# Two wide output projections: from three column pieces of 384, 384 and 256 to two of 512

## The chip, the cores and the metric

The kernel runs on one core of a Trainium2 chip. The metric is the device time of one execution in microseconds (us). Besides the timed runs there is one execution taken by the hardware profiler; its rows are what every argument here goes by.

Engines are named as the profile names them: PE is the matrix engine (TensorE) and PEld its weight loads, ACT is ScalarE, DVE is VectorE, POOL is GpSimd, SP is the engine whose queue issues nearly all transfers.

## The reference, cut to what matters

One step of an encoder layer for 1024 prompt tokens and 64 sample tokens, width 1024, all in float32:

```
h   = rms_norm(x, n_pre)
aq, af, ai, ag, bq, bk, bv, bg, cu, cg = split(h @ w_in)
a_out = rms_norm(hgrn2_scan(aq, af, ai)) * silu(ag)        # width 512
b_out = stick_breaking_attention(bq, bk, bv) * silu(bg)    # width 256
c_out = pool_mix(cu) * silu(cg)                            # width 256
mix = concat(a_out, b_out, c_out) @ w_out                  # 1024 x 1024
x   = x + rms_norm(mix, n_post)
q   = rms_norm(x, nx_pre) @ w_xq                           # 4 heads of 256
p   = softmax(q k_mem / 16) per head, over 256 memory rows
x   = x + rms_norm(concat(p v_mem) @ w_xo, nx_post)        # 1024 x 1024
```

The two "wide" products of the title are `mix @ w_out` and the last one with `w_xo`. Each maps 1088 token rows of width 1024 to 1024 columns.

## The kernel before, in words

**Precision.** A float32 product is made of three matmuls. Every operand is kept as a high part `hi` (rounded by ACT to the type float32r) and a low part `lo` (DVE subtracts `hi` from the original); the product is hi*hi + hi*lo + lo*hi, accumulated in PSUM. `mm3` issues these three for each of the 8 blocks of 128 along the inner dimension (`k`).

**Token tiles and chunks.** There are nine token tiles: eight of 128 prompt rows, and tile 8 with the 64 sample rows. In projections with the tokens as the streamed operand they go in three chunks of 384, 384 and 320 tokens (`CHUNKS`). The normalised, transposed input lies in six token buffers, a pair `hhi0..2`, `hlo0..2` of the shape 128 x 8 x n for n = 384, 384, 320. Two sets of them exist in the course of the program: one for `h`, later one for the second norm's output.

**Wide projections.** Here the tokens are the stationary operand: `side(i)` splits tile i of the mixed heads `C` into `whi`, `wlo`, and asks for the residual rows to be loaded into `C`. `wide(i)` streams the weights against them, one PSUM bank per piece of columns. The weights live in the six token buffers once the last projection of a chunk has read them: the piece of the columns 0:384 in pair 0, 384:768 in pair 1, 768:1024 in pair 2. `load_wide` fills one pair: for each block of 128 columns one transfer of 512 KB into a staging buffer `wraw` (the pool has two, shared with the norms), one ACT copy (hi), one DVE subtraction (lo). A tile needs 8 x 3 = 24 matmuls per piece, 72 in all. For tile 8 `whi` and `wlo` stand side by side in the 128 stationary columns, so it takes two matmuls per `k`, 48 in all. `wide_norm` then reads each piece from PSUM: an ACT square with a sum per row, a DVE multiplication by the gain; POOL adds the pieces' sums and makes the reciprocal root; DVE adds the result to the residual in `C`.

**Where this stands.** `w_out` is loaded during the last keys/values block of the stick-breaking attention (`keys_values`, j = 1), chunk by chunk; its tiles run partly between the attention's last units (task "sb", names `sm`, `wT`, `vb`) and mostly after them. `w_xo` is loaded during the last head (h = 3) of the cross attention, again chunk by chunk; its tiles are the end of the program, in the order 0 to 5, 8, 6, 7.

**What sets the order.** The program is one generator (`main`) and side tasks spawned from it. A planner (`Sched`) with a cost in us for every instruction runs the first task in its list whose inputs are ready when PE gets there; a wide projection gives way to other tasks after each six matmuls. The tile framework then places the instructions on each engine; blocks under `urgent()` have higher priority. Each engine runs its own list strictly in that order. The helper lines that carry nearly everything are `mm` (L171 before), `act` (L183), `tt` (L187), `stt` (L191) and `wload` (L286).

Of the kernel before, what the change touches and what calls it, by code (L numbers as in the profile page):

```python
# [8 lines left out]
F32 = mybir.dt.float32  # L9
# [6 lines left out]
P = 128  # L16
# [7 lines left out]
EPS = 1e-6  # L24
QSCALE = 128 ** -0.5
NEG = -1e30
PIECES = ((0, 3), (3, 6), (6, 8))
CHUNKS = ((0, 384), (384, 384), (768, 320))
URGENT = 1500
TABLE = {AF.Exp: 0, AF.Sigmoid: 2, AF.Ln: 5, AF.Silu: 18}  # L30
# [74 lines left out]
def hybrid_step(  # L105
# [627 lines left out]
    def main():  # L733
# [208 lines left out]
            yield from pooled(1, us[1])  # L942

        st, sbops = {}, {}
        wo, wdeps = [], []

        def keys_values(bi, j, wbs, q):


            kh = pool([P, KEYS], F32R, "kh", 2)  # L950
            kl = pool([P, KEYS], F32R, "kl", 2)
            ck = pool([P, P], F32, "ck", 1)
            SP.dma_start(ck, cache_sb_k[j * P:(j + 1) * P, :])
            split(ck, kh[:, SEQ:SEQ + P], kl[:, SEQ:SEQ + P])
            vb = pool([P, NT, P], F32, "vb", 2)
            cv = pool([P, P], F32, "cv", 2)
            SP.dma_start(cv, cache_sb_v[0, 0, :, 2 * j:2 * j + 2, :])
            sbops[j] = (q, (kh, kl), vb, cv)
            rows, cs = slice(j * P, (j + 1) * P), slice(j * P, (j + 1) * P)
            for c, (t0, n) in enumerate(CHUNKS):  # L960
                n1 = min(n, SEQ - t0)
                sch.fresh(**wbs[0][2])
                yield None
                yield from proj(wbs[0], c, hT)
                o = cur["o"]
                kr = pool([P, 384], F32, "kr", 3)
                with urgent():
                    split(o[:, :n1], kh[:, t0:t0 + n1], kl[:, t0:t0 + n1])
                    if n1 < n:
                        split(o[:, n1:n], kh[:, SEQ + P:], kl[:, SEQ + P:])  # L970
                    act(kr[:, :n], o[:, :n], AF.Copy)
                SP.dma_start(p_sb_k[rows, t0:t0 + n1], kr[:, :n1])
                if n1 < n:
                    SP.dma_start(s_sb_k[rows, :], kr[:, n1:n])
                sch.fresh(**wbs[1][2])
                yield None
                yield from proj(wbs[1], c, hT)
                o = cur["o"]
                vr = pool([P, 384], F32, "kr", 3)
                with urgent():  # L980
                    act(vr[:, :n], o[:, :n], AF.Copy)

                def values_tm(vr, c, t0, n, n1):
                    yield None
                    if c:
                        yield f"bv{j}{c - 1}"
                    pt = ps_tp().rearrange("p (c t) -> p c t", t=P)
                    i0, full = t0 // P, n1 // P
                    for i in range(full):
                        tr(pt[:, i, :], vr[:, i * P:(i + 1) * P], P)  # L990
                    if n1 < n:
                        tr(pt[:SMP, full, :], vr[:, n1:n], P)
                    act(vb[:, i0:i0 + full, :], pt[:, :full, :], AF.Copy)
                    SP.dma_start(p_sb_v[0, 0].rearrange("(i p) h d -> p i (h d)", p=P)[:, i0:i0 + full, cs],
                                 vb[:, i0:i0 + full, :])
                    if n1 < n:
                        act(vb[:SMP, 8, :], pt[:SMP, full, :], AF.Copy)
                        SP.dma_start(s_sb_v[0, 0].rearrange("p h d -> p (h d)")[:, cs], vb[0:SMP, 8, :])
                sch.spawn(values_tm(vr, c, t0, n, n1), f"bv{j}{c}")
                if (j, c) == (0, 0):  # L1000
                    sch.spawn(sb_all(sbops, pool), "sb")
                if j == 1:
                    b0, b1 = PIECES[c]
                    pair = [big([P, KT, n], F32R, f"{x}{c}") for x in ("hhi", "hlo")]
                    wdeps.append(load_wide(w_out, pair, range(b0, b1)))
                    wo.append((slice(b0 * P, b1 * P), *pair))
                elif c == 1:
                    prefetch(bi + 2)
                    prefetch(bi + 3)

        def load_wide(src, tiles, blocks):
            save, sch.cur = sch.cur, Sched.Task(None, "w")
            hi, lo = tiles
            for i, cb in enumerate(blocks):
                with urgent():
                    raw = wload(src[cb])
                    cs = slice(i * P, (i + 1) * P)
                    act(hi[:, :, cs], raw, AF.Copy)
                    sub(lo[:, :, cs], raw, hi[:, :, cs].bitcast(F32))
            dep, sch.cur = dict(sch.cur.dep), save  # L1020
            return dep
        for bi, (kind, j) in enumerate(names):
            if (kind, j) == ("cu", 0):
                wbs = [wq.pop(bi), wq.pop(bi + 1)]
# [175 lines left out]
                SP.dma_start(C[:n, i].rearrange("p k t -> p (k t)"), res)  # L1200
            return ahi, alo, dict(sch.cur.dep)

        def wide(i, sd, w, wdeps, bank):

            ahi, alo, dep = sd
            pp = []
            for (cs, whi, wlo), wd in zip(w, wdeps):
                sch.fresh(**dep)
                sch.cur.dep.update(wd)
                yield None  # L1210
                p = bank()
                wn = cs.stop - cs.start
                if i < 8:
                    yield from mm3(p[:, :wn], [(ahi[:, k], alo[:, k], whi[:, k, :wn], wlo[:, k, :wn])
                                               for k in range(KT)], 6)
                else:
                    for k in range(KT):
                        mm(p[:, :wn], ahi[:, k], whi[:, k, :wn], k == 0, False)
                        mm(p[:, :wn], ahi[:, k], wlo[:, k, :wn], False, k == KT - 1)
                        if k % 3 == 2:  # L1220
                            yield None
                pp.append((cs, p[:, :wn]))
            cur["pp"] = pp

        def wide_norm(i, pp, gain):
# [22 lines left out]
        for i in range(NT):  # L1248
            sch.fresh()
            yield ("sb", 0, i)  # L1250
            yield ("sb", 1, i)
            sd = side(i, xrows(i))
            if i == NT - 1:
                xw[0] = wblock(w_xq[0])
            yield from wide(i, sd, wo, wdeps, ps_mm if i < 8 else ps_hg)
            if i == NT - 1:
                xw[1] = wblock(w_xq[1])
            with urgent():
                x = wide_norm(i, cur["pp"], g2)
            SP.dma_start(x1d[i * P:i * P + _rows(i), :], x)  # L1260
            sch.done[("x1", i)] = max(sch.cur.dep.values())
            if not h2 and "sb" in sch.done:
                open_h2()
# [62 lines left out]
            sch.done[("cross", h, c)] = max(sch.cur.dep.values())  # L1326

        prev = None
        wx, wdeps = [], []
        for h in range(4):  # L1330
            def load_kv(h):
                kr = xq([P, 2, NMEM], F32, "kraw", 1)
# [16 lines left out]
            for c, (t0, n) in enumerate(CHUNKS):  # L1349
                n1 = min(n, SEQ - t0)  # L1350
                qhi = xq([P, 2, 384], F32R, "qhi", 2)
                qlo = xq([P, 2, 384], F32R, "qlo", 2)
                qs = xq([P, 2, SMP], F32, "qs", 2) if n1 < n else None
                deps = {}
                for dt in range(2):
                    sch.fresh(**wbs[dt][2])
                    yield ("h2", c)
                    yield from proj(wbs[dt], c, hT)
                    o = cur["o"]
                    with urgent():  # L1360
                        act(qhi[:, dt, :n1], o[:, :n1], AF.Copy, scale=0.0625)
                        stt(qlo[:, dt, :n1], o[:, :n1], 0.0625, qhi[:, dt, :n1].bitcast(F32), ALU.mult, ALU.subtract)
                        if n1 < n:
                            tsc(qs[:, dt, :], o[:, n1:n], 0.0625, ALU.mult)
                    if c == 2 and h < 3:
                        xw[2 * h + 2 + dt] = wblock(w_xq[2 * h + 2 + dt])
                if h == 3:
                    b0, b1 = PIECES[c]
                    pair = [h2p([P, KT, n], F32R, f"{x}{c}") for x in ("hhi", "hlo")]
                    wdeps.append(load_wide(w_xo, pair, range(b0, b1)))  # L1370
                    wx.append((slice(b0 * P, b1 * P), *pair))
                if prev is not None:
                    save = dict(sch.cur.dep)
                    yield prev
                    sch.fresh(**save)
                sch.spawn(cross(h, c, qhi, qlo, qs, kv), f"cross{h}{c}")
                prev = f"cross{h}{c}"
# [3 lines left out]
        for i in (0, 1, 2, 3, 4, 5, 8, 6, 7):  # L1381
            sch.fresh()
            yield ("cross", 3, i // 3)
            sd = side(i, x1d[i * P:i * P + _rows(i), :])
            yield from wide(i, sd, wx, wdeps, ps_mm)
            x = wide_norm(i, cur["pp"], g4)
            for cs, _ in cur["pp"]:
                SP.dma_start(yrows(i)[:, cs], x[:, cs])
# [71 lines left out]
```

## Time and profile before

| | us |
|---|---|
| three timed runs | 934.79, 938.41, 1758.64; median 938.41 |
| the profiled execution, its own time | 935.02 |
| its span, first to last instruction | 933.3 |
| outside the span | 1.7 |
| granted TensorE clock, mean | 0.996 |

One of the three runs is far off the other two; the profiled execution stands beside the lower of those two. In the rows below a time is counted in us from the span's start. Matmuls are pipelined and their ends are modelled, so the duration in a matmul's row is longer than what one costs in a stream: that is read from the starts of successive matmuls. A row of the timeline gives the start, the duration (all in us), the engine, the line, what it writes and reads, and in square brackets the idle time of the engine ahead of it with what ended it.

### The profile page before, as it was taken

To read this page: it belongs to the slowest core of one execution; us is meant where nothing else is said; L and a number is where in the kernel's file an instruction comes from. 1 tells how busy PE (TensorE), PEld (TensorE's weight loads), DVE (VectorE), ACT (ScalarE), POOL (GpSimd) and SP (SyncE) were. 2 spreads that over 40 slices of the span, in tenths; PEclk is the share of its full clock that TensorE was granted. 3 is DMA by queue.
4 is the path that set the end of the run, shared out by engine and by line. 5 is a ranking of instruction groups with operands and counts; after the bars stand their busy time and mean duration, and the time that the engine had idled before them with its cause. 6 is when DMAs were issued, how large, how long until landed. Compare 5 with 4: busy or idle time off the path is not lost.

```text
span 933.3 us, 18372 instructions
## 1 busy us (share of the span) xinstructions
PE 914.2 (98%) x7504; PEld 853.6 (91%) x7504; DVE 556.6 (60%) x1125; ACT 479.5 (51%) x1005; POOL 107.2 (11%) x194
## 2 busy tenths in 40 slices
PE   8899999999999999999999999999999999999997
PEld 7899999999998999989779788999999999999997
DVE  6849483674678574552684777565564545563343
ACT  7623384658767774963673765433452333342231
POOL 5502430010010010000000000211200000001110
PEclk9999999999999999999999999999999999999999
DMA  8815511011100111012111411222433111232231
GB/s 306 259 38 181 142 46 47 25 49 29 47 27 31 47 33 46 25 47 79 47 31 36 157 61 69 90 68 80 164 119 92 30 39 46 76 106 91 91 101 58
DMA packets 33126, 73.60 MB, mean 79 GB/s; under 512 B 5601, under 2 KB 18065, under 8 KB 33042
## 3 DMA queue, kind: packets, MB, share of 16 engines
q1 hardware_dynamic: 30112, 68.07, 22.7%
q0 software_dynamic: 1888, 4.35, 1.3%
q8 instruction: 59, 0.97, 0.4%
q14 instruction: 25, 0.20, 0.1%
q10 hardware_dynamic: 1042, 0.01, 0.1%
HBM read 56.45 MB, written 15.89 MB: 78 GB/s over the span
## 4 chain that ended last, share of the span: by engine, by line
PE 82%; DVE 6%; ACT 4%; DMA 4%; issue 2%; POOL 1%; DVEq 0%; POOLq 0%; ACTq 0%
PE mm L171 64%; PE hg L171 14%; PE tp L175 5%; DVE sm L650 3%; DVE sm L187 1%; DVE wlo L187 1%; ACT L183 1%; ACT whi L183 1%; DMA xt<-in_x_prompt_dram 1%; DVE hlo L187 1%; DMA wraw<-in_w_xk_dram 1%; DMA mkd<-mraw 1%; DMA wraw<-in_w_xo_dram 1%; DMA gT<-in_norm_mem_dram 1%; DMA mvd<-mtm 1%
## 5 line engine op out<-in xcount | busy, mean ns | idle before, releaser
L171 PE MATMUL mm<-hhi,whi 128*128 128x384 f32 (+2 forms) x1272 | 425.1, 334 | 0.0
L171 PE MATMUL mm<-hlo,whi 128*128 128x384 f32 (+2 forms) x1272 | 412.5, 325 | 0.0
L171 PE MATMUL mm<-hhi,wlo 128*128 128x384 f32 (+2 forms) x1248 | 405.3, 325 | 0.0
L171 PEld LDWEIGHTS mm<-hhi,whi 128*128 128x128 f32 x1272 | 239.2, 188 | 6.3 <-issue 1.3
L171 PEld LDWEIGHTS mm<-hlo,whi 128*128 128x128 f32 x1272 | 239.5, 188 | 1.2 <-issue 0.9
L171 PEld LDWEIGHTS mm<-hhi,wlo 128*128 128x128 f32 x1248 | 234.6, 188 | 0.4 <-issue 0.3
L187 DVE TENSOR_TENSOR wlo<-wraw,whi 128x1024 fp32r<-128x1024 f32 (+1 forms) x53 | 63.5, 1200 | 56.6 <-ACT whi L183 56.3
L183 ACT ACT_TABLE_LOAD x66 | 84.7, 1283 | 19.0 <-DVE E L187 12.0
L183 ACT ACTIVATE whi<-wraw 128x1024 fp32r<-128x1024 f32 (+1 forms) x53 | 55.3, 1043 | 71.5 <-PE mm L171 54.7
L183 ACT ACTIVATE wraw<-mm 128x384 f32<-128x384 f32 (+3 forms) x51 | 22.9, 449 | 72.8 <-PE mm L171 62.9
L650 DVE TENSOR_TENSOR_SCAN sm<-sm 128x384 f32<-128x384 f32 (+4 forms) x52 | 48.3, 938 | 14.0 <-ACT sm L183 14.0
L183 ACT ACTIVATE sm<-hg 128x384 f32<-128x384 f32 (+4 forms) x104 | 42.2, 485 | 15.7 <-PE hg L171 8.7
L187 DVE TENSOR_TENSOR wraw<-mm,gain 128x384 f32<-128x384 f32 (+1 forms) x48 | 24.4, 510 | 41.6 <-ACT wraw L183 41.3
L1241 POOL TENSOR_TENSOR small<-small 128x1 f32<-128x1 f32 (+1 forms) x18 | 4.2, 234 | 375.3 <-ACT wraw L183 375.3
L183 ACT ACTIVATE E<-E 128x512 f32<-128x512 f32 (+1 forms) x68 | 32.8, 515 | 10.5 <-DVE E L187 9.9
L171 PE MATMUL mm<-mhi,wlo 128*128 128x256 f32 x128 | 35.8, 289 | 1.8 <-DVE wlo L187 1.8
L321 POOL TENSOR_TENSOR small<-small,mhalf 128x1 f32<-128x1 f32 (+2 forms) x50 | 36.0, 719 | 4.2
L171 PE MATMUL mm<-mhi,whi 128*128 128x256 f32 x128 | 36.2, 293 | 0.1
L171 PE MATMUL mm<-mlo,whi 128*128 128x256 f32 x128 | 35.1, 283 | 0.0
L443 POOL COPY qf<-q 128x512 f32<-128x512 f32 (+1 forms) x12 | 14.6, 1218 | 177.6 <-PE hg L171 140.7
L187 DVE TENSOR_TENSOR wlo<-C,whi 128x1024 fp32r<-128x1024 f32 x16 | 19.6, 1225 | 24.9 <-ACT whi L183 23.4
L191 DVE SCALAR_TENSOR_TENSOR C<-wraw,small,C 128x384 f32<-128x384 f32 (+3 forms) x54 | 27.8, 569 | 10.2 <-POOL small L321 10.2
(209 smaller groups left out, 1409.1 us busy)
## 6 DMA issues: line engine op xcount, KB each, us to landing
wraw<-in_w_in_dram SPq DMA_DIRECT2D x28, 512.0 KB, 3.6
xt<-in_x_prompt_dram SPq DMA_DIRECT2D x8, 512.0 KB, 6.5
wraw<-in_w_xv_dram SPq DMA_DIRECT2D x8, 512.0 KB, 3.9
wraw<-in_w_out_dram SPq DMA_DIRECT2D x8, 512.0 KB, 3.6
C<-in_x_prompt_dram SPq DMA_DIRECT2D x8, 512.0 KB, 3.5
x1d<-C SPq DMA_DIRECT2D x8, 512.0 KB, 2.8
wraw<-in_w_xq_dram SPq DMA_DIRECT2D x8, 512.0 KB, 3.6
wraw<-in_w_xo_dram SPq DMA_DIRECT2D x8, 512.0 KB, 3.6
```

The lines of the kernel that those rows point to most:

```text
L171: cur['PE'] = PE.matmul(out, lhsT=lhsT, rhs=rhs, start=start, stop=stop, skip_group_check=True)
L175: PE.transpose(out, in_, ident[:n, :n])
L183: cur['ACT'] = ACT.activation(out, in_, func, **kw)
L187: cur['DVE'] = DVE.tensor_tensor(out=out, in0=a, in1=b, op=op)
L191: DVE.scalar_tensor_tensor(out=out, in0=a, scalar=s, in1=b, op0=op0, op1=op1)
L321: POOL.tensor_tensor(out=r[:n, :w], in0=r[:n, :w], in1=mhalf[:n, :w], op=ALU.pow)
L443: POOL.tensor_copy(qf[:, 1, :], qq)
L650: DVE.tensor_tensor_scan(m[:nq, :n][:, ::-1], m[:nq, :n][:, ::-1], m[:nq, :n][:, ::-1], 1.0 if p is None else p[:nq, 0:1], ALU.mult, ALU.min)
L1241: POOL.tensor_tensor(out=ms[:n, 0:1], in0=ms[:n, 0:1], in1=ms[:n, pi:pi + 1], op=ALU.add)
```

## The change

Both wide projections take two pieces of 512 columns ("halves") in place of three. A half needs 8 rows (k = 0..7) of 512 weights for the hi part and as many for the lo part; the 16 rows of the two halves are laid one behind the other into the same six token buffers. Pair 0 (8 x 384 = 6 x 512) takes the rows k = 0..5 of half 0; pair 1 the rows 6, 7 of half 0 and 0..3 of half 1; pair 2 the rows 4..7 of half 1. `ROWS` says so, as (half, k from, k to, first row in the buffer). Each entry of `ROWS` is loaded with four transfers, one per block of 128 columns, which carry only the rows of that entry: 384 KB each for pair 0, 128 KB and then 256 KB for pair 1, 256 KB for pair 2. That is 16 transfers, 16 ACT copies and 16 DVE subtractions per weight matrix where there were 8 of each, on the same number of elements. A half of tile 0 cannot end before every row of that half is there: half 0 reads pairs 0 and 1, half 1 reads pairs 1 and 2.

A tile takes 2 x 24 = 48 matmuls of 512 columns, tile 8 takes 32. `wide_norm` is unchanged but now gets two pieces: two squares, two multiplications, two residual additions, and no separate addition of sums on POOL (L1241). The results leave in two transfers per tile, not three.

```
-PIECES = ((0, 3), (3, 6), (6, 8))
+ROWS = (((0, 0, 6, 0),), ((0, 6, 8, 0), (1, 0, 4, 2)), ((1, 4, 8, 0),))
...
-        def load_wide(src, tiles, blocks):
+        def load_wide(src, w, tiles, c):
             save, sch.cur = sch.cur, Sched.Task(None, "w")
-            hi, lo = tiles
-            for i, cb in enumerate(blocks):
-                with urgent():
-                    raw = wload(src[cb])
-                    cs = slice(i * P, (i + 1) * P)
-                    act(hi[:, :, cs], raw, AF.Copy)
-                    sub(lo[:, :, cs], raw, hi[:, :, cs].bitcast(F32))
+            for half, k0, k1, r0 in ROWS[c]:
+                rows = [t.rearrange("p k n -> p (k n)")[:, r0 * 512:(r0 + k1 - k0) * 512].rearrange(
+                    "p (k n) -> p k n", n=512) for t in tiles]
+                hi, lo = rows
+                for i in range(4):
+                    with urgent():
+                        raw = wpool([P, KT, P], F32, "wraw", 2)[:, :k1 - k0]
+                        SP.dma_start(raw, src[4 * half + i][:, k0:k1])
+                        cs = slice(i * P, (i + 1) * P)
+                        act(hi[:, :, cs], raw, AF.Copy)
+                        sub(lo[:, :, cs], raw, hi[:, :, cs].bitcast(F32))
+                for k in range(k0, k1):
+                    w[half][k] = (hi[:, k - k0], lo[:, k - k0], dict(sch.cur.dep))
...
-        def wide(i, sd, w, wdeps, bank):
+        def wide(i, sd, w, bank):
             ahi, alo, dep = sd
             pp = []
-            for (cs, whi, wlo), wd in zip(w, wdeps):
+            for half in range(2):
                 sch.fresh(**dep)
-                sch.cur.dep.update(wd)
+                for _, _, wd in w[half]:
+                    for e, v in wd.items():
+                        sch.cur.dep[e] = max(v, sch.cur.dep.get(e, 0.0))
                 yield None
                 p = bank()
                 if i < 8:
-                    yield from mm3(p[:, :wn], [(ahi[:, k], alo[:, k], whi[:, k, :wn], wlo[:, k, :wn])
-                                               for k in range(KT)], 6)
+                    yield from mm3(p, [(ahi[:, k], alo[:, k], w[half][k][0], w[half][k][1]) for k in range(KT)], 6)
```

Because the planner sees other costs, instructions also change places. Two places are shown, each before and after; in the changed file `mm` is L172, `act` L184 and transposes L176. A number behind a name tells one buffer from another of the same name.

**PE, where the last keys projection ends and the attention's last units follow.** Before: `hhi_6193` and `hlo_6194` are the second piece of `w_out`, streamed for tile 0; `kh`, `qh` are keys and queries of an attention unit with 512 keys; `negmask` is its mask.

```order
L171 MATMUL mm<-hhi_6193,whi 128x384
L171 MATMUL mm<-hlo_6194,whi 128x384
L171 MATMUL mm<-hhi_6193,wlo 128x384
L171 MATMUL hg<-kh,qh 128x512 x2
L171 MATMUL hg<-kl,qh 128x512 x2
L171 MATMUL hg<-kh,ql 128x512 x2
L171 LDWEIGHTS identb
L171 MATMUL hg<-negmask,identb 128x128
```

After, the same unit; `hhi_109` is still the token buffer of the projection, `tp<-ident,kr` the transposes of its result.

```order
L172 MATMUL mm<-hhi_109,wlo 128x320
L172 MATMUL hg<-kh,qh 128x512 x2
L172 MATMUL hg<-kl,qh 128x512 x2
L172 MATMUL hg<-kh,ql 128x512 x2
L176 MATMUL tp<-ident,kr 128x128 x2
L176 MATMUL tp<-ident,kr 64x128
L172 LDWEIGHTS identb
L172 MATMUL hg<-negmask,identb 128x128
```

Before, 36 wide matmuls of tile 0 stand between the projection and this unit; now the unit follows the projection at once, and tile 0's matmuls stand in groups of six between this and the following units, 36 of its 48 in all; the last 12 come behind the last unit.

**ACT, from the loading of the third pair for `w_xo` to the first tile's square.** Before: `hhi_9460` is pair 2, `e` the exponentials of the softmax, `PTh` and `PTs` copies of the transposed weights, `wraw,small<-mm` the square of a piece.

```order
L183 ACTIVATE whi<-C 128x1024
L183 ACTIVATE qhi<-mm 128x256
L183 ACTIVATE hhi_9460<-wraw 128x8x128 x2
L183 ACTIVATE e,small<-hg,small 128x256 x2
L183 ACTIVATE e,small<-hg,small 64x256
L183 ACTIVATE wraw,small<-mm 128x384
L183 ACTIVATE PTh<-tp 128x256 x2
```

After: `hhi_9099` is pair 1 and `hhi_9261` pair 2.

```order
L184 ACTIVATE whi<-C 128x1024
L184 ACTIVATE qhi<-mm 128x256
L184 ACTIVATE hhi_9099<-wraw 128x4x128 x2
L184 ACTIVATE e,small<-hg,small 128x256 x2
L184 ACTIVATE e,small<-hg,small 64x256
L184 ACTIVATE hhi_9261<-wraw 128x4x128 x2
L184 ACTIVATE PTh<-tp 128x256 x2
L184 ACTIVATE PTs<-tp 128x64 x2
L184 ACTIVATE hhi_9261<-wraw 128x4x128 x2
L184 ACTIVATE wraw,small<-mm 128x512
```

Where the two copies of pair 2 stood, the last two of pair 1 stand now; the four copies of pair 2 follow behind the exponentials, two of them behind the copies `PTs`.

More of the change, by code (lines that the diff above doesn't have):

```diff
@@ L944, in main @@
         st, sbops = {}, {}
-        wo, wdeps = [], []
+        wo = [[None] * KT, [None] * KT]
         def keys_values(bi, j, wbs, q):
@@ L1002, in keys_values @@
                 if j == 1:
[L1003 to L1006, printed above, removed]
+                    load_wide(w_out, wo, [big([P, KT, n], F32R, f"{x}{c}") for x in ("hhi", "hlo")], c)
                 elif c == 1:
@@ L1009, in keys_values @@
                     prefetch(bi + 3)
-        def load_wide(src, tiles, blocks):
+        def load_wide(src, w, tiles, c):
             save, sch.cur = sch.cur, Sched.Task(None, "w")
-            hi, lo = tiles
-            for i, cb in enumerate(blocks):
-                with urgent():
-                    raw = wload(src[cb])
-                    cs = slice(i * P, (i + 1) * P)
-                    act(hi[:, :, cs], raw, AF.Copy)
-                    sub(lo[:, :, cs], raw, hi[:, :, cs].bitcast(F32))
-            dep, sch.cur = dict(sch.cur.dep), save
-            return dep
+            for half, k0, k1, r0 in ROWS[c]:
[11 more added lines that the diff above has]
+                    w[half][k] = (hi[:, k - k0], lo[:, k - k0], dict(sch.cur.dep))
+            sch.cur = save
         for bi, (kind, j) in enumerate(names):
@@ L1201, in side @@
             return ahi, alo, dict(sch.cur.dep)
-        def wide(i, sd, w, wdeps, bank):
+        def wide(i, sd, w, bank):
             ahi, alo, dep = sd
             pp = []
-            for (cs, whi, wlo), wd in zip(w, wdeps):
+            for half in range(2):
                 sch.fresh(**dep)
-                sch.cur.dep.update(wd)
+                for _, _, wd in w[half]:
+                    for e, v in wd.items():
+                        sch.cur.dep[e] = max(v, sch.cur.dep.get(e, 0.0))
                 yield None
                 p = bank()
-                wn = cs.stop - cs.start
                 if i < 8:
-                    yield from mm3(p[:, :wn], [(ahi[:, k], alo[:, k], whi[:, k, :wn], wlo[:, k, :wn])
-                                               for k in range(KT)], 6)
+                    yield from mm3(p, [(ahi[:, k], alo[:, k], w[half][k][0], w[half][k][1]) for k in range(KT)], 6)
                 else:
                     for k in range(KT):
-                        mm(p[:, :wn], ahi[:, k], whi[:, k, :wn], k == 0, False)
-                        mm(p[:, :wn], ahi[:, k], wlo[:, k, :wn], False, k == KT - 1)
+                        mm(p, ahi[:, k], w[half][k][0], k == 0, False)
+                        mm(p, ahi[:, k], w[half][k][1], False, k == KT - 1)
                         if k % 3 == 2:
                             yield None
-                pp.append((cs, p[:, :wn]))
+                pp.append((slice(512 * half, 512 * half + 512), p))
             cur["pp"] = pp
@@ L1254, in main @@
                 xw[0] = wblock(w_xq[0])
-            yield from wide(i, sd, wo, wdeps, ps_mm if i < 8 else ps_hg)
+            yield from wide(i, sd, wo, ps_mm if i < 8 else ps_hg)
             if i == NT - 1:
@@ L1328, in main @@
         prev = None
-        wx, wdeps = [], []
+        wx = [[None] * KT, [None] * KT]
         for h in range(4):
@@ L1367, in main @@
                 if h == 3:
[L1368 to L1371, printed above, removed]
+                    load_wide(w_xo, wx, [h2p([P, KT, n], F32R, f"{x}{c}") for x in ("hhi", "hlo")], c)
                 if prev is not None:
@@ L1384, in main @@
             sd = side(i, x1d[i * P:i * P + _rows(i), :])
-            yield from wide(i, sd, wx, wdeps, ps_mm)
+            yield from wide(i, sd, wx, ps_mm)
             x = wide_norm(i, cur["pp"], g4)
```

## The prediction

> **What bounds the kernel now.** I read the page's busy shares first, then the chain that ended last, then who waits for whom on PE.
>
> ```profile
> PE 914.2 (98%) x7504; PEld 853.6 (91%) x7504; DVE 556.6 (60%) x1125; ACT 479.5 (51%) x1005; POOL 107.2 (11%) x194
> PE 82%; DVE 6%; ACT 4%; DMA 4%; issue 2%; POOL 1%; DVEq 0%; POOLq 0%; ACTq 0%
> PE tp L175 <- DVE sm L187: 2.3, 3, 1.3
> ```
>
> PE is the bound, and its longest wait sums to 2.3 us over the whole span. So only PE's own work, or a wait that did not exist, moves the time. But busy shares are averages, so I ask for the stretches that the change touches. The columns are: stretch, length, then busy us (and instructions) of PE, PEld, DVE, ACT, POOL, clock, DMA share and GB/s.
>
> ```profile
> core 0: us, PE busy (x) PEld busy (x) DVE busy (x) ACT busy (x) POOL busy (x), PEclk, DMA share, GB/s
> 517.00:547.40 30.40, 29.42 (x242) 21.88 (x243) 27.25 (x50) 22.95 (x59) 0.00 (x0) 1.00 0.33 106
> 547.40:554.20 6.80, 6.80 (x41) 6.33 (x39) 4.16 (x5) 4.28 (x8) 0.00 (x0) 1.00 0.33 105
> 554.20:576.10 21.90, 21.58 (x205) 16.84 (x204) 16.98 (x28) 14.98 (x37) 0.20 (x1) 1.00 0.00 1
> 836.00:915.00 79.00, 79.00 (x513) 79.00 (x512) 31.35 (x55) 19.58 (x54) 11.18 (x22) 1.00 0.26 87
> ```
>
> The last row is the final projection: PE 79.00 of 79.00, all others under 40%. There the price of a matmul in a stream is the time, and anything saved on ACT, DVE or POOL is worth nothing. In the first row, the attention's units beside the loading of w_out, DVE has 27.25 of 30.40: work added to DVE can be felt there. From 554.2 to 576.1 the attention's last units and tile 0 of w_out share PE.
>
> **What 512 columns cost.** Durations of matmuls overlap, so I count starts: the first rows of successive pieces, for a tile of w_xo (841 to 852) and the last piece of one of w_out (584 to 587); then twelve matmuls of 320 columns between two starts (811 to 813); then passes of 512 columns in the attention, each two concurrent matmuls.
>
> ```profile
> 584.56 0.28 PE L171 MATMUL mm<-hhi,whi 128*128 128x256 f32 x1
> 587.28 0.33 PE L171 MATMUL mm<-hhi,whi 128*128 128x384 f32 x1
> ...
> 841.22 0.34 PE L171 MATMUL mm<-hhi,whi 128*128 128x384 f32 x1
> 849.55 0.28 PE L171 MATMUL mm<-hhi,whi 128*128 128x256 f32 x1
> 852.42 0.34 PE L171 MATMUL mm<-hhi,whi 128*128 128x384 f32 x1
> ...
> 811.86 0.31 PE L171 MATMUL mm<-hhi,whi 128*128 128x320 f32 x1
> 813.61 0.28 PE L171 MATMUL hg<-KTh,qhi 128*128 128x256 f32 x1
> ...
> 562.06 0.40 PE L171 MATMUL hg<-kl,qh 64*128 64x512 f32 x2
> 562.29 0.40 PE L171 MATMUL hg<-kh,ql 64*128 64x512 f32 x2
> ```
>
> 48 matmuls of 384 take 8.33 us, 0.1735 each; 24 of 256 take 2.87, 0.1196 each, in w_xo, and 2.72, 0.1133 each, in w_out; 12 of 320 take 1.75, 0.1458 each. From 256 to 320 to 384 each 64 columns add 0.026 and 0.028 us, so 512 is 0.1735 + 2 x 0.027 = 0.2275 us, my value. The bounds: 0.222 below, since the attention's 512-column pass starts 0.23 apart at the timeline's rounding; above, plain proportion, 0.1735 x 512/384 = 0.2313.
>
> A tile of w_xo is now 8.33 + 2.87 = 11.20 us, and becomes 48 x 0.2275 = 10.92: 0.28 saved. A tile of w_out is 8.33 + 2.72 = 11.05: 0.13 saved. Tile 8 is two thirds: 32 x 0.1735 + 16 x 0.1196 = 7.47 against 32 x 0.2275 = 7.28, 0.19 saved in w_xo and 0.09 in w_out. The sum: 8 x 0.28 + 8 x 0.13 + 0.28 = **3.6 us saved**. By 0.222 a tile is 10.66 and the sum 8.2; by 0.2313 it is 11.10 and the sum 0.5.
>
> Matmuls fall from (8 x 72 + 48) x 2 = 1248 to 832; 3.6 us is 0.009 for each of the 416 that go. The Trainium skill, page "TensorE: Matmul & The Clock Gate", section "Back-to-back issue gap", gives a gap of N/2.4 + 2.5 ns for an isolated stream on the full clock; by it 416 matmuls are worth 416 x 2.5 ns = 1.0 us, an estimate from that page. The trace has 173.5 ns at 384 columns where the page has 162.5, so I keep the trace.
>
> **What loading costs.** Elements are the same, instructions double. The rows for 1024, 512 and 256 elements, ACT and then DVE, and the transfers by size:
>
> ```profile
> L183 ACT ACTIVATE hhi<-wraw 128x1024 fp32r<-128x1024 f32 x16 | 16.3, 1054 | 2.7 <-DMA wraw<-in_w_xo_dram 2.2 <-DMA wraw<-in_w_out_dram 0.4
> L183 ACT ACTIVATE hhi<-tp 128x512 fp32r<-128x512 f32 x16 | 8.9, 596 | 12.6 <-PE tp L175 12.6
> L183 ACT ACTIVATE wraw<-mm 128x256 f32<-128x256 f32 x16 | 5.9, 370 | 4.6 <-PE mm L171 4.6
> L187 DVE TENSOR_TENSOR hlo<-wraw,hhi 128x1024 fp32r<-128x1024 f32 x16 | 19.1, 1222 | 9.2 <-ACT hhi L183 9.2
> L187 DVE TENSOR_TENSOR hlo<-tp,hhi 128x512 fp32r<-128x512 f32 x16 | 10.5, 686 | 9.4 <-ACT hhi L183 9.4
> L187 DVE TENSOR_TENSOR wraw<-mm,gain 128x256 f32<-128x256 f32 x16 | 6.7, 419 | 4.4 <-ACT wraw L183 4.4
> ...
> wraw<-in_w_xo_dram SPq DMA_DIRECT2D x8, 512.0 KB, 3.6
> kraw<-mkd SPq DMA_DIRECT2D x4, 256.0 KB, 3.0
> out_dram<-C SPq DMA_DIRECT2D x8, 128.0 KB, 2.3
> ```
>
> Pair 1 on DVE: 4 x 0.419 + 4 x 0.686 = 4.42 us against 3 x 1.222 = 3.67, so 0.75 more; on ACT 4 x 0.370 + 4 x 0.596 = 3.86 against 3.16. For w_out this falls into 517 to 547, where DVE is nearly full: it costs between nothing (PE has the projection as filler) and 0.75; I take **0.5**. Pair 0 adds 0.1 to 0.2 per engine; for w_out it falls into 500 to 517, ahead of that row, and I cost it at nothing.
>
> **The attention's last units.** The order moves 36 wide matmuls from ahead of the 512-key unit to between the units after it.
>
> ```profile
> 556.02 1.22 DVE L650 TENSOR_TENSOR_SCAN sm<-sm 128x512 f32<-128x512 f32 x1 [2.60 <-ACT sm L183]
> ```
>
> The unit's first scan began at 556.0, behind 6.8 us of wide matmuls. Now its scores can start at 547.4, but ACT and DVE first split tile 1 and half of pair 2, until about 551, so DVE begins some 4.5 us earlier. It pays two subtractions of 0.686 inside the chain, and each group of six is 6 x 0.2275 = 1.37 us where it was 1.04 or 0.70. PE's own count: 28.7 us from 547.4 to 576.1 held all 72 matmuls of tile 0; it will hold 36 (8.2 us), so 28.7 - 11.05 + 8.2 = 25.9, ending near 573.3, and the last 12 (2.7 us) end near 576.0. So the move is neutral; the units now have little cover if DVE is late. I take **0.5** lost, between 3 gained (two thirds of DVE's 4.5 us are kept) and 2 lost (over half of the 3.3 us by which six groups of 1.37 exceed two of 1.04 and four of 0.70, if they hold the units up).
>
> **The weights of w_xo.** Here a new wait can arise: half 1 of tile 0 needs all of pair 2, and pair 1 now takes eight transfers through two staging buffers, ahead of it.
>
> ```profile
> 812.44 2.00 ACT L183 ACTIVATE hhi<-wraw 128x1024 fp32r<-128x1024 f32 x2
> 821.10 0.71 SPq L286 DMA_DIRECT2D wraw<-in_w_xo_dram  x1
> 825.93 1.06 ACT L183 ACTIVATE hhi<-wraw 128x1024 fp32r<-128x1024 f32 x1 [1.38 <-DMA wraw<-in_w_xo_dram]
> 827.03 1.22 DVE L187 TENSOR_TENSOR hlo<-wraw,hhi 128x1024 fp32r<-128x1024 f32 x1 [0.44 <-ACT hhi L183]
> 826.46 0.34 PE L171 MATMUL mm<-hhi,whi 128*128 128x384 f32 x1
> 838.36 0.28 PE L171 MATMUL mm<-hhi,whi 128*128 128x256 f32 x1
> ```
>
> Before, pair 2 was complete at 828.25 and first read at 838.36: 10.1 us in hand. After, on the same clock: pair 1 comes free at 812.4; the first two blocks lie ready and are done at 812.44 + 0.37 + 2 x 0.42 = 813.65. Five rounds of two follow: one of 128 KB, 2.3 + 0.37 + 2 x 0.42 = 3.5 us, and four of 256 KB, 3.0 + 0.60 + 2 x 0.69 = 5.0 each. Done at 837.1. PE: from 826.46 to 838.36 are 11.90 us, of which 42 matmuls of 384 are 7.29; the other 4.61 are the cross attention. The six matmuls ahead of 826.46 go too (1.06), so PE reaches pair 2 at 825.40 + 4.61 + 36 x 0.2275 = 838.2. One us in hand, but each round also queues behind other work on ACT, DVE and SP, where each engine keeps its order: behind a late copy on ACT stand the `PTh` copies that PE waits for. I take **0.5** lost. The ends: nothing; and rounds as long as today's (3.6 + 1.05 + 1.22 = 5.9): 813.65 + 5 x 5.9 = 843.2, 5.0 late. For w_out the same chain ends near 556, long before the 12 last matmuls: nothing.
>
> **The end.** After the last matmul stand one square, the root, the residual and the output.
>
> ```profile
> 927.23 0.38 ACT L183 ACTIVATE wraw<-mm 128x256 f32<-128x256 f32 x1 [2.28 <-PE mm L171]
> 928.84 1.54 DVE L191 SCALAR_TENSOR_TENSOR C<-wraw,small,C 128x384 f32<-128x384 f32 x3 [0.68 <-POOL small L321]
> ```
>
> The square grows from 0.37 to 0.60 (the 512 rows above), the residual is two of about 0.73 for 1.54 us, and the last transfer doubles (2.3 to 3.0 at most): **0.3** lost, between 0 and 0.8. All other evacuations, 18 POOL additions and 16 more loads and 9 fewer stores on SP lie under a full PE and cost nothing; if a late load removed that cover, the price is the one above.
>
> **The sum**, against the profiled execution's 935.0: -3.6 + 0.5 + 0.5 + 0.5 + 0.3 = -1.8, **933.2 us**. That execution lies 3.4 below the median of the runs, 938.4, whose ordinary runs are 934.8 and 938.4.
>
> **Rivals.**
> - *Late weights*: w_xo's rounds keep today's 5.9 us. PE stands 5.0 us at 838: 935.0 - 3.6 + 1.0 + 5.0 + 0.3 = 937.7, slower than before. It decides from 2.3 us of lateness on, where it eats the 3.6 less the other losses. For it: ACT stood 1.38 for such a load and the one at 821.10 took 4.8 us to land. Against: the blocks are half as large. Chance 0.15.
> - *Attention drawn forward*: the units' earlier start is kept, 3 us: 935.0 - 3.6 + 0.5 - 3.0 + 0.5 + 0.3 = 929.7. For it: 4.5 us earlier on DVE. Against: PE was 21.58 of 21.90 busy there. 0.15.
> - *The matmul's price goes with its columns*, so that nothing is saved by fewer of them: 935.0 - 0.5 + 1.8 = 936.3. For it: the rows give three widths, none at 512 with full height, and 256 has two prices. The page's small gap points the same way; by its 1.0 us saved the time would be 935.8, an estimate. 0.15.
> - My forecast, 930 to 935.5: 0.53. The last 0.02 is for anything beyond 2%.
>
> **Range and chances.** The lower rival with a little of the better pace reaches 928; late weights, with the spread of ordinary runs, 940. Of these runs about 2% can be told from no change, some 19 us; no case comes near it. Faster by over 2%: 0.02; within: 0.96; slower: 0.02.
>
> **What would show it.** Starts of 512-column matmuls 0.2275 apart at the end of the program and nine last tiles in 8 x 10.92 + 7.28 us show the pace; idle time on PE at the first matmul that reads pair 2 for w_xo, put down to ACT or DVE `hhi`, `hlo`, shows late weights; tile 0 of w_out finished well before 576 shows the attention drawn forward. It is wrong if a step apart from these gains or loses over 5 us, say transfers of 1 KB rows that land later than 128 KB does now.

## The result, and the profile after

| | before | changed |
|---|---|---|
| median of five runs, us | 934.79 | 942.33 |
| the profiled execution, its own time | 935.02 | 943.14 |
| its span | 933.3 | 941.4 |

The ratio of the runs is 1.0083, with a 95% interval of 1.0068 to 1.0097: slower by about 7.5 us. That is under the 2% of the chances above, but more than the ordinary runs of either kernel differ among themselves, and outside the forecast (933.2, range 928 to 940). One run before (1758.64 us) and one of a later experiment (2225.2) stand far off all others and are not in the ratios.

The page of the changed kernel gives the busy time of each engine. PE has 416 matmuls fewer and less busy time, but a smaller share of a longer span.

```profile
PE 912.3 (97%) x7088; PEld 815.1 (87%) x7088; DVE 553.1 (59%) x1103; ACT 478.3 (51%) x983; POOL 100.4 (11%) x176
```

So PE waits. Who it waits for between 500 and 945 us, before and then after (line and tile that waits, who ends the wait, us in total, times, longest):

```profile
PE tp L175 <- DVE sm L187: 1.0, 2, 0.6
PE hg L171 <- DVE qlo L191: 0.8, 1, 0.8
```

```profile
PE tp L176 <- DVE wraw L192: 8.4, 8, 1.1
PE tp L176 <- DVE sm L188: 1.8, 5, 0.5
PE hg L172 <- DVE qlo L192: 1.3, 1, 1.3
```

The first row after is new: eight waits of about 1.05 us, once per tile of `w_out` behind the attention. The stretch 576 to 690 us, before and then after (length, then busy us and instructions of PE, PEld, DVE, ACT, POOL, clock, DMA share, GB/s), says the same: PE is idle for 0.65 us of 114 before, and for 8.4 after.

```profile
576.00:690.00 114.00, 113.35 (x747) 112.30 (x747) 65.58 (x107) 47.55 (x113) 22.68 (x44) 1.00 0.33 112
```

```profile
576.00:690.00 114.00, 105.62 (x497) 86.24 (x496) 56.90 (x73) 42.21 (x84) 18.48 (x36) 1.00 0.29 99
```

What waits are the transposes of the second norm's output (task `prep_h2`): after a tile's residual is added, ACT squares the row, POOL makes the root, DVE writes the normalised rows to `wraw`, and PE transposes them, eight at a time. Before and then after, on PE, for two successive tiles:

```profile
646.93 1.04 PE L175 MATMUL tp<-ident,wraw 128*128 128x128 f32 x8
...
658.86 1.03 PE L175 MATMUL tp<-ident,wraw 128*128 128x128 f32 x8
```

```profile
598.16 1.07 PE L176 MATMUL tp<-ident,wraw 128*128 128x128 f32 x8 [1.04 <-DVE wraw L192]
...
611.47 1.06 PE L176 MATMUL tp<-ident,wraw 128*128 128x128 f32 x8 [1.05 <-DVE wraw L192]
```

A tile's period is 658.86 - 646.93 = 11.93 us before and 611.47 - 598.16 = 13.31 after. The chain that these transposes wait for, from the copy `whi` that PE's end of a tile releases to the norm's output, before and then after (timelines of ACT, DVE and POOL, put in order of time):

```profile
636.65 1.06 ACT L183 ACTIVATE whi<-C 128x1024 fp32r<-128x1024 f32 x1
...
643.59 1.29 DVE L191 SCALAR_TENSOR_TENSOR wraw<-C,small,gain 128x1024 f32<-128x1024 f32 x1 [2.23 <-POOL small L321]
```

```profile
603.24 1.06 ACT L184 ACTIVATE whi<-C 128x1024 fp32r<-128x1024 f32 x1 [3.32 <-PE mm L172]
...
604.20 0.58 ACT L184 ACTIVATE wraw<-mm 128x512 f32<-128x512 f32 x1
...
604.97 0.75 POOL L321 TENSOR_SCALAR small<-small 128x1 f32<-128x1 f32 x1 [8.28 <-ACT wraw L184]
...
606.40 1.42 DVE L192 SCALAR_TENSOR_TENSOR C<-wraw,small,C 128x512 f32<-128x512 f32 x2 [0.24 <-POOL small L322]
...
607.90 1.06 ACT L184 ACTIVATE wraw<-C 128x1024 f32<-128x1024 f32 x1 [3.03 <-issue]
...
610.04 1.29 DVE L192 SCALAR_TENSOR_TENSOR wraw<-C,small,gain 128x1024 f32<-128x1024 f32 x1 [2.23 <-POOL small L322]
```

It takes 643.59 + 1.29 - 636.65 = 8.23 us before and 610.04 + 1.29 - 603.24 = 8.09 after: two pieces didn't make it longer. Before, its result lay ready at 644.88, 2.05 us ahead of the transposes at 646.93; after, PE stands at the transposes before it is there. They have been moved in PE's order. Before, the transposes shown stand 66 wide matmuls behind the end of their tile (48 x 0.1735 + 18 x 0.1147 = 10.4 us). Of the other prompt tiles one more has 66, two have 72 and one has only 42; the first and the last stand far later. After, the eight that wait have 30, but one of them 26. For the tile of the chain above, the first matmul behind its end and the last one ahead of the transposes are:

```profile
603.27 0.40 PE L172 MATMUL mm<-hhi,whi 128*128 128x512 f32 x1
...
610.04 0.39 PE L172 MATMUL mm<-hhi,wlo 128*128 128x512 f32 x1
```

With the last one counted these are 30, 30 x 0.2333 = 7.0 us, and the chain takes 8.1: about 1.1 us are missing, which is the wait.

**Why they moved.** The order comes from the planner's clock, and the change has one line that touches it which is not about pieces. Before, `wide` writes the time at which the weights are ready over the tile's own (`sch.cur.dep.update(wd)`); the time at which `side` has split the tile is thereby lost, and in the planner's book a tile's matmuls start at once. The change keeps the later of the two (`max(v, ...)`). In the planner's book PE then stands some 5 us, by its own costs, at every tile for that split, though on the chip it doesn't; its clock runs ahead, and the norm's output seems ready after fewer matmuls. The transposes are listed earlier, and in the built order they stand at 30. So for this move the sentence on the change above, "Because the planner sees other costs", named the wrong cause: it is this line. The first of the two places shown there goes with it too, as the second experiment shows.

The second thing to see is the pace. Two starts on PE with 42 equal matmuls between them in a tile of `w_out`, and two with 44 in one of `w_xo`:

```profile
599.30 0.40 PE L172 MATMUL mm<-hlo,whi 128*128 128x512 f32 x1
...
609.10 0.39 PE L172 MATMUL mm<-hlo,whi 128*128 128x512 f32 x1
```

```profile
859.76 0.39 PE L172 MATMUL mm<-hhi,whi 128*128 128x512 f32 x1
...
869.74 0.39 PE L172 MATMUL mm<-hhi,wlo 128*128 128x512 f32 x1
```

9.80 / 42 = 0.2333 us in `w_out`, 9.98 / 44 = 0.2268 in `w_xo`, at the same clock.

### The profile page after: what moved, and what is told of

Read it like the earlier page. It is cut to its first block, busy times and chain, and to the rows that moved or that the text cites. A ratio compares the mean times of both kernels' runs of the same rounds, so it can differ in the third digit from the quotient of the medians.

```text
span 941.4 us, 17497 instructions
## 1 busy us (share of the span) xinstructions
PE 912.3 (97%) x7088; PEld 815.1 (87%) x7088; DVE 553.1 (59%) x1103; ACT 478.3 (51%) x983; POOL 100.4 (11%) x176
## 5 line engine op out<-in xcount | busy, mean ns | idle before, releaser
L172 PE MATMUL mm<-hhi,whi 128*128 128x384 f32 (+2 forms) x1136 | 402.6, 354 | 0.0
L172 PE MATMUL mm<-hlo,whi 128*128 128x384 f32 (+2 forms) x1136 | 390.4, 344 | 0.0
L172 PE MATMUL mm<-hhi,wlo 128*128 128x384 f32 (+2 forms) x1120 | 384.1, 343 | 0.0
L172 PEld LDWEIGHTS mm<-hhi,whi 128*128 128x128 f32 x1136 | 213.4, 188 | 16.4 <-issue 0.9
L172 PEld LDWEIGHTS mm<-hlo,whi 128*128 128x128 f32 x1136 | 213.6, 188 | 12.7 <-issue 1.5
L172 PEld LDWEIGHTS mm<-hhi,wlo 128*128 128x128 f32 x1120 | 210.3, 188 | 10.6
L184 ACT ACTIVATE whi<-wraw 128x1024 fp32r<-128x1024 f32 (+1 forms) x53 | 55.3, 1043 | 67.3 <-PE mm L172 56.1
L321 POOL TENSOR_SCALAR small<-small 128x1 f32<-128x1 f32 (+1 forms) x18 | 11.9, 663 | 458.5 <-ACT wraw L184 458.5
L184 ACT ACTIVATE sm<-hg 128x384 f32<-128x384 f32 (+4 forms) x104 | 42.1, 482 | 12.5 <-PE hg L172 5.3
L184 ACT ACTIVATE whi<-C 128x1024 fp32r<-128x1024 f32 (+1 forms) x18 | 18.2, 1012 | 57.0 <-PE mm L172 57.0
L184 ACT ACTIVATE wraw<-mm 128x512 f32<-128x512 f32 (+1 forms) x34 | 20.1, 591 | 41.3 <-PE mm L172 25.4
L172 PE MATMUL mm<-mhi,wlo 128*128 128x256 f32 x128 | 36.0, 289 | 2.3 <-DVE wlo L188 2.3
L184 ACT ACTIVATE E<-E 128x512 f32<-128x512 f32 (+1 forms) x68 | 32.8, 515 | 10.5 <-DVE E L188 10.0
L172 PE MATMUL mm<-mhi,whi 128*128 128x256 f32 x128 | 35.7, 288 | 0.6 <-ACT whi L184 0.6
L184 ACT ACTIVATE hhi<-tp 128x512 fp32r<-128x512 f32 (+1 forms) x36 | 18.9, 570 | 33.1 <-PE tp L176 33.0
L172 PE MATMUL mm<-mlo,whi 128*128 128x256 f32 x128 | 35.1, 283 | 0.0
L188 DVE TENSOR_TENSOR wraw<-mm,gain 128x512 f32<-128x512 f32 x32 | 21.9, 686 | 22.0 <-ACT wraw L184 21.9
```

The costliest lines, as they stand in the source:

```text
L172: cur['PE'] = PE.matmul(out, lhsT=lhsT, rhs=rhs, start=start, stop=stop, skip_group_check=True)
L184: cur['ACT'] = ACT.activation(out, in_, func, **kw)
L188: cur['DVE'] = DVE.tensor_tensor(out=out, in0=a, in1=b, op=op)
L321: POOL.tensor_scalar(out=r[:n, :w], in0=ms, scalar1=more, scalar2=EPS, op0=ALU.add, op1=ALU.add)
```

## The experiments

`w_out` alone in two pieces was not run; it could have told where the gain comes from that the sum below leaves without a place. Two questions: is it the one line of bookkeeping or the pieces that make the wait, and what makes the two paces? Times ahead of 547 us wander: the last matmul of the last keys projection starts at 547.25 in the profiled execution before, at 548.13 after, and between 546.20 and 549.41 in seven more with the same order up to there. Where two profiles are compared below, I count from that matmul to the end of the span: 933.3 - 547.25 = 386.1 before, 941.4 - 548.13 = 393.3 after, 7.2 more.

### Only `w_xo` in two pieces

```
-                    wdeps.append(load_wide(w_xo, pair, range(b0, b1)))
+                    load_rows(w_xo, wx, [...], c)        # the change's load_wide
-            yield from wide(i, sd, wx, wdeps, ps_mm)
+            yield from wide_rows(i, sd, wx, ps_mm)       # the change's wide
```

> Only w_xo goes in two pieces of 512 columns; w_out keeps its three pieces and the order around it. Theory (what the change lost, it lost around w_out, where the transposes of the second norm now stand ahead of their input): nothing of the 8.4 us wait is left, and the price of 512 columns, 0.227 us in w_xo, saves 0.28 us a tile, 8 x 0.28 + 0.19 = 2.4 us, less 0.3 at the end: about 933 us against a profiled 935.0, a ratio near 0.9975. Rival (the loss comes with rows over the buffers as such, the late weights among it): w_xo's part would cost as w_out's did, some 4 to 8 us, a ratio of 1.004 or more.

Measured: 933.72 us against 934.69, ratio 0.9989 (0.9978 to 1.0001); from the last keys matmul to the end 931.3 - 547.35 = 384.0, 2.1 less than before. There is no wait for the norm. The gain in the profile is the 2.1 expected; the runs show half of it, with an interval that reaches from all of it to nothing. The rival is out: what the change lost, it did not lose in `w_xo` or in the laying of rows.

### The change with the planner's word as before

```
-                        sch.cur.dep[e] = max(v, sch.cur.dep.get(e, 0.0))
+                        sch.cur.dep[e] = v
```

> The change with one word of its planner bookkeeping as it was before: in wide() the time at which the weights are ready takes the place of the time at which the tile's own split is ready, where the change takes the later of the two. In PE's order the transposes of the second norm's output then stand at least 42 wide matmuls behind the end of their tile, but for one at 36, where the change has 36 for all. Theory: the chain from a tile's last matmul to the norm's output takes 36 x 0.2335 + 1.05 = 9.5 us, and 42 matmuls are 9.8, so the wait of 8.4 us falls to that of the one tile, 1.05; the time is 942.3 - 7.3 = 935 us, a ratio to before of 1.000. Rival A (the chain itself is what grew, by the larger squares and copies, and waits wherever the transposes stand): 940 or more, the wait still there. Rival B (the loss is the slower pace of 512 columns in w_out and the loading, not the wait): 941.

Measured: 937.06 us, ratio 1.0024 (1.0010 to 1.0038), where the change has 1.0083. PE's waits between 500 and 945:

```profile
PE tp L176 <- DVE sm L188: 4.6, 4, 3.3
PE hg L172 <- DVE PTl L188: 0.5, 1, 0.5
```

The wait for the norm is gone, the one tile at 36 matmuls included, so rivals A and B fall. The expectation had counted 36 for the change too, where it has 30; its chain of 9.5 us is therefore too long, and 30 x 0.2335 + 1.05 gives 8.1, as measured above. That is why 36 are enough. But some 2 us of the gain did not come. The word moves the attention too: 30 wide matmuls stand ahead of the 512-key unit again, and the next transposes of weights on PE wait 3.3 us for DVE's `sm`. That wait was not foreseen.

### The same, with the left half of SBUF 64 bytes further

```
-        ident = const([P, P], F32, "ident")
+        ident = const([P, P], F32, "ident"); POOL.memset(const([P, 16], F32, "shift"), 0.0)
```

> The kernel of the run before this, with an unused block of 64 bytes a partition among the constants, which moves the attention's half of SBUF, the six token buffers of w_out among it, by 64 bytes; the order of all engines is the same. In the change the weights of w_out begin 32 bytes past a multiple of 128, those of w_xo 96 past one; here both 96. Theory (the place of the streamed operand sets the pace): 512 columns in w_out take 0.227 us as in w_xo, in place of 0.2335, 416 x 0.0067 = 2.8 us less than without the block, and w_xo stays at 0.227. Rival (w_out is slower because of what runs beside it, the norms' copies and transfers): 0.2335 stays and the time with it.

Measured: 933.72 us, ratio 0.9990 (0.9979 to 1.0001), 3.3 less than the run before. 512 columns in `w_out` go from 0.2333 to 0.2267, in `w_xo` they stay. 2.8 us were expected of it. The order of PE, ACT, DVE and SP is the same in both, so the pace goes with the place in SBUF of what was moved, not with what runs beside it.

### The kernel before, with the change's word

```
-                sch.cur.dep.update(wd)
+                sch.cur.dep.update({e: max(v, sch.cur.dep.get(e, 0.0)) for e, v in wd.items()})
```

> The kernel before, in three pieces, with the change's one word of planner bookkeeping: the later of the weights' and the split's time is taken for a wide piece. The transposes then stand 39 matmuls of 384 columns behind the end of their tile, 39 x 0.1735 = 6.8 us, where the kernel before has 60 or 66 (9.7 to 10.4). Theory (this word makes the wait, not the two pieces): the chain takes about 9.5 us, so PE waits some 2.7 us in each of eight tiles, 20 us: 950 to 957, slower than the change itself. Rival (the two pieces make the wait, by their longer squares and copies): the wait is under 0.5 us a tile and the time 935 to 938.

Measured: 949.89 us, ratio 1.0158 (1.0137 to 1.0179), with three pieces throughout.

```profile
PE tp L175 <- DVE wraw L191: 11.9, 8, 1.6
```

```profile
628.25 1.06 PE L175 MATMUL tp<-ident,wraw 128*128 128x128 f32 x8 [1.53 <-DVE wraw L191]
...
642.03 1.06 PE L175 MATMUL tp<-ident,wraw 128*128 128x128 f32 x8 [1.40 <-DVE wraw L191]
```

The word alone puts the same wait into the kernel before and costs it more than the whole change did. The size was 1.5 us a tile, not 2.7: the chain of 9.5 us rested on the same false count of 36. 39 x 0.1735 + 1.5 = 8.3 agrees with a chain of 8.1 to 8.2. The period is 13.78 against 11.93; 1.85 x 8 = 14.8 of the 15 us.

### The planner's word switched behind the attention

```
-    ... = max(v, sch.cur.dep.get(e, 0.0))
+    ... = max(v, sch.cur.dep.get(e, 0.0)) if "sb" not in sch.done else v
```

> The change with the planner's word switched only once the attention is done: until then the later of the two times counts, as in the change, and the order up to the attention's last unit is the change's, row for row; after it the weights' time counts, and the transposes of a tile's norm stand 48 wide matmuls behind its end, where the change has 36. Theory: 48 matmuls are 48 x 0.2335 = 11.2 us, more than the chain's 9.5, so the 8.4 us wait goes whole, and the 3.3 us at the attention's last units that the overwriting kernel paid does not come: 942.3 - 8.4 = 934, a ratio near 0.999. Rival (the wait goes somewhere else, to the transposes of the last two tiles ahead of the first projection of the cross attention): 936 to 938.

Measured: 932.21 us, ratio 0.9970 (0.9952 to 0.9988): faster than before, and 10 us faster than the change, whose pieces, loading and order up to the attention it has.

```profile
620.84 1.03 PE L176 MATMUL tp<-ident,wraw 128*128 128x128 f32 x8
...
632.92 1.03 PE L176 MATMUL tp<-ident,wraw 128*128 128x128 f32 x8
```

No idle time stands in these rows; the period is 12.08, where the change has 13.31. The transposes stand 42 wide matmuls behind the end of their tile, not 48 as expected, and 42 x 0.2333 = 9.8 us are still more than the chain. Counted from the last keys matmul it is 929.2 - 546.20 = 383.0, 10.3 less than the change. A tile gives 1.23 of it, which is more than the 1.05 that PE stood idle: the last matmul ahead of a stop takes the whole 0.39 of its row, one in a stream 0.2333. Eight tiles are 9.8; the wait of 1.3 for `qlo` is gone as well, and a new one of 0.5 for `PTl` has come.

### The same, shifted by 64 bytes on the left

> The kernel of the run before this with the unused 64 bytes that shift the left half of SBUF. Theory (the place sets the pace): 0.227 in w_out, 416 x 0.0067 = 2.8 us less, about 931, a ratio near 0.996. Rival (the norm's chain is again late, since 48 matmuls now pass in 10.9 us): a wait of up to 0.5 us a tile and no gain.

Measured: 929.06 us, ratio 0.9936 (0.9919 to 0.9953): the fastest of all, some 6 us under the kernel before.

```profile
622.26 1.03 PE L176 MATMUL tp<-ident,wraw 128*128 128x128 f32 x8
...
634.03 1.03 PE L176 MATMUL tp<-ident,wraw 128*128 128x128 f32 x8
```

```profile
600.28 0.39 PE L172 MATMUL mm<-hhi,whi 128*128 128x512 f32 x1
...
609.80 0.39 PE L172 MATMUL mm<-hhi,whi 128*128 128x512 f32 x1
```

The period is 11.77, and 42 matmuls take 9.52, 0.2267 each. The norm's chain still ends in time, though the transposes stand 42 matmuls behind their tile and not the 48 that the rival names. The edit is the planner's line of the run before and the block of the first shift.

### Shifted by 64 bytes on the right side instead

```
+        ... POOL.memset(wpool([P, 16], F32, "shift"), 0.0)
```

> The same kernel, with 64 unused bytes on the right side of SBUF instead: the stationary tiles whi and wlo and the weights of w_xo begin 32 past a multiple of 128 in place of 96, while the weights of w_out stay at 32. Theory A (the pace is set by the place of the streamed operand against that of the stationary one, 0 apart in w_xo and 64 apart in w_out): now both are 0 apart, 0.227 in both projections, about 931. Theory B (it is set by the place of the streamed operand alone): w_out stays at 0.2335 and w_xo becomes 0.2335 too, 416 x 0.0067 = 2.8 us more than without the block, about 937.

Measured: 935.38 us, ratio 1.0004 (0.9990 to 1.0018). Two starts in a tile of `w_xo`, 44 matmuls apart:

```profile
859.45 0.39 PE L172 MATMUL mm<-hhi,whi 128*128 128x512 f32 x1
...
869.71 0.39 PE L172 MATMUL mm<-hhi,wlo 128*128 128x512 f32 x1
```

10.26 / 44 = 0.2332: now `w_xo` has the slow pace as well, and `w_out` keeps it. The time is that of theory B. But the edit does not do all that the expectation says: as built, the block lies just below `wraw`, `whi` and `wlo`, and these three stay where they were, 224 past a multiple of 256 bytes; only the weights of `w_xo` move, from 224 to 160. So both projections now have the streamed operand 64 bytes apart from the stationary one, and theory A asks for the slow pace in both as well. The two theories are not separated, and no run moved the stationary tiles.

### Other shifts

The block of the left shift is 8, 24, 32 and 48 floats wide in place of 16:

```
+        ... POOL.memset(const([P, 8], F32, "shift"), 0.0)      # 24, 32, 48
```

> The same kernel with 32 unused bytes on the left: the weights of w_out begin at a multiple of 64. Theory (a start at a multiple of 64 saves a part of a line at each end): 512 columns in w_out take less than the 0.227 of w_xo. Rival (the distance to the stationary tile counts, now 32 where it was 64): between 0.227 and 0.2335. The cross attention's operands move too.

> The kernel with the late transposes, the left half of SBUF shifted by 96 bytes: the weights of w_out start at a multiple of 256. One look, for the pace alone: 0.2267 or 0.2333; starts of 160, 192 and (on the right) 160 past a multiple of 256 gave 0.2333, 224 gave 0.2267.

> The same with a shift of 128 bytes: a start of 32 past a multiple of 256. If the pace repeats every 128 bytes it is that of 160: 0.2333.

> The same with a shift of 192 bytes: a start of 96 past a multiple of 256. If the pace repeats every 128 bytes it is that of 224: 0.2267, and the time some 929 to 931; if it repeats every 256 bytes or goes by something else, 0.2333 and 932 to 934.

Measured: 932.67 us (ratio 0.9976, 0.9959 to 0.9994) for 32 bytes; single profiled times of 934.17, 929.44 and 933.00 for 96, 128 and 192. The paces, each the mean of the starts of like matmuls in a row, with gaps of over 1.25 medians left out (`whi` and `wlo` start at 224 in all of them):

| start, bytes past a multiple of 256 | us for 512 columns | where |
|---|---|---|
| 0 | 0.2332 | `w_out`, shift 96 |
| 32 | 0.2291 | `w_out`, shift 128 |
| 96 | 0.2322 | `w_out`, shift 192 |
| 160 | 0.2333 | `w_out`, no shift; `w_xo`, shift 64 on the right |
| 192 | 0.2333 | `w_out`, shift 32 |
| 224 | 0.2267 | `w_out`, shift 64; `w_xo`, elsewhere |

Both of my guesses fall: a start at a multiple of 64 saves nothing, and the pace does not repeat every 128 bytes (32 and 160 differ, 96 and 224 too). Nor are there only two paces. No rule is settled by these six starts, and each can be read as a distance to the stationary tiles as well.

### The kernel before, shifted by 64 bytes

The edit is that of the first left shift, 16 floats.

> The kernel before with the 64 unused bytes on the left, nothing else. Theory (the start of the streamed operand sets the pace, and 256 columns go the other way: 0.1147 where the buffers start 160 past a multiple of 256 bytes, 0.1194 where they start 224 past one): w_out's last piece rises to 0.1194, (8 x 24 + 16) x 0.0047 = 1.0 us more, so the shift by itself is no gain: 934 to 937, a ratio of 1.000 to 1.002. Rival (the shift helps for another reason, whatever the pieces): 932 or less.

Measured: 936.13 us against 935.01, ratio 0.9997 (0.9978 to 1.0015); the medians' own is 1.0012, and the interval holds both. 256 columns in `w_out` rose from 0.1147 to 0.1192. The shift is no gain in itself; where 512 columns gain by it, 256 lose. The 0.1147 is a mean: in the profile before, at one and the same start, a piece of 24 takes 0.1135 each (584.56 to 587.17) and another 0.1178 (608.70 to 611.41). For 256 columns something besides the place counts, and it stays open; with the shift no such piece is below 0.118.

## Why the prediction was wrong

**The cover.** The step that failed is "All other evacuations [...] lie under a full PE and cost nothing". It held for each length but not for the order: PE's list has transposes in it that wait for the end of just these evacuations, the norm's output. Before, that output was 2.05 us early in the tile shown above, and not early at all in the tightest, whose transposes stand only 42 matmuls behind it; the DVE row and the PE rows of the kernel before:

```profile
618.54 1.28 DVE L191 SCALAR_TENSOR_TENSOR wraw<-C,small,gain 128x1024 f32<-128x1024 f32 x1 [1.03 <-POOL small L321]
```

```profile
619.51 0.34 PE L171 MATMUL mm<-hhi,wlo 128*128 128x384 f32 x1
619.97 1.06 PE L175 MATMUL tp<-ident,wraw 128*128 128x128 f32 x8
```

618.54 + 1.28 = 619.82, and PE starts 0.15 later. That is no cover: in the change, where PE waits, it starts as long behind DVE's end (610.04 + 1.29 = 611.33, 611.47). PE stood idle from 619.85 to 619.97 here, too short a stop for the row to show it. So the kernel before was at the edge already, and the profile said so. I had looked for moved instructions at two places, the attention and the loading of `w_xo`, and not in the tiles of `w_out` between them. No rival named this wait. Without the wait the change measured 2.8 us under before, where the forecast has 1.8; that this is near is partly luck, since the next term has the wrong sign in `w_out` and the sum below leaves 1.7 us of gain without a place. That the word of bookkeeping makes it and not the pieces is shown from both sides: three pieces with the word wait 11.9 us, two pieces without it don't wait.

**The price of 512 columns.** In `w_xo` it is 0.2268 where I had 0.2275, and that part alone gave the 2.1 us in the profile that follow from 8 x 0.28 + 0.19 - 0.3. In `w_out` the term was mis-sized, past its bound of 0.2313: 48 x 0.2333 = 11.20 against 8.33 + 24 x 0.1147 = 11.08 before, so 0.12 a tile is lost where 0.13 should be saved, about 1.0 us over all tiles in place of -1.1. The two prices of 256 columns, which I noted, were the sign that a width has no single price; I took one for both all the same. The rival by which the price goes with the columns (0.2313) is nearer in `w_out` and wrong in `w_xo`. The Trainium skill's isolated gap (page "TensorE: Matmul & The Clock Gate", section "Back-to-back issue gap") would be 512 / 2.4 + 2.5 = 216 ns, an estimate; the traces have 227 to 233 and decide.

**The attention's last units.** Right: forecast to end 25.9 us behind the projection, and the last unit's matmuls start 573.68 - 548.13 = 25.6 behind it. Tile 1 begins 28.6 us behind it, 28.9 before: 0.3 gained, where I had 0.5 lost.

**The weights of `w_xo`.** Right, and the 0.5 was not needed. The last subtractions for pair 2, and the first matmul that reads it:

```profile
846.37 1.28 DVE L188 TENSOR_TENSOR hlo<-wraw,hhi 128x512 fp32r<-128x512 f32 x2
```

```profile
848.88 0.39 PE L172 MATMUL mm<-hhi,whi 128*128 128x512 f32 x1
```

Ready at 847.65, read at 848.88: 1.2 us in hand, where 837.1 and 838.2 had left 1.1. The rival of late weights did not happen.

**Loading `w_out`.** The 0.5 stays open: the change and the kernel with the late word, alike up to there, reach the end of the projection 1.9 us apart, far more than the term.

**The end.** From the last wide matmul's start to the end 6.63 us against 6.40: 0.2 lost, 0.3 forecast.

**The sum.** Counted from the last keys matmul, the change is 7.2 longer than before. The run with the planner's word switched behind the attention divides this: the word there costs 10.3 (393.3 against 383.0), and all the rest of the change gains 3.1 (383.0 against 386.1). Of the 3.1, `w_xo` with its end gave 2.1 in its own experiment and the attention 0.3; the pace in `w_out` should have cost 1.0, so some 1.7 of gain is not placed. The 0.9 ahead of the last keys matmul is within what that stretch wanders by.

## What to carry to other kernels

When a change passes through a planner, read every line that feeds the planner's clock as a change of its own, and follow PE's order to each instruction that waits for another engine: for each, take from the trace how long its input lies ready before it is used. Here nothing to 2.05 us was the cover in the tiles shown, and one `max` took it away. A saving of 0.1 to 0.3 us a tile is smaller than a move by one group of six matmuls. Price a matmul by a row with the same buffer, not only the same width. When an experiment moves a buffer, look up where each operand lies in the built program, not where the edit was meant to put it.

## What the runs showed of the hardware

The pace of a stream of float32r matmuls changed with where in a partition of SBUF the streamed operand starts: 0.2267 to 0.2333 us for 512 columns, 3%, with the order, the stationary tiles and the clock unchanged, and it moves with the buffer (64 bytes on the left speed up `w_out` alone, 64 on the right slow down `w_xo` alone). 256 columns go the other way at the same two starts, 0.1147 on average and 0.1194. Whether the start itself counts or its distance to the stationary tiles, why, and with what period, is open. The Trainium skill (page "SBUF — State Buffer", section "Operand start alignment") gives rules on where an operand may start and says that they are about legality, not speed; here a start that is legal throughout changes the speed. Over 416 matmuls it was worth about 3 us, as much as the change itself could have saved.
